# Hybrid attention kernel: row maxima one product a step, their transposition a step later, block ends copied once or on two engines

## The chip, the cores and the metric

The kernel runs on one NeuronCore of a Trainium2 chip. The metric is the device time of one execution in microseconds (us). The core has five engines with queues of their own: TensorE (PE in the rows; PEld is its weight load), VectorE (DVE), ScalarE (ACT), GpSimd (POOL) and SyncE (SP), which issues most DMAs. TensorE writes its products into PSUM, a memory of eight banks, from which VectorE and ScalarE read them.

## The reference

Two layers of a trunk, each with four parallel head groups: grouped-query attention (4 heads of 64), gated linear attention, latent attention (MLA, 4 heads) and a Mamba-2 scan, then one output projection. The change touches only the softmax attention of the first and third group:

```python
def one_block(qblk):
    s = jnp.einsum('bqhgd,bkhd->bhgqk', qblk, k, preferred_element_type=F32) * scale
    p = jax.nn.softmax(s, axis=-1)
    return jnp.einsum('bhgqk,bkhd->bqhgd', p.astype(v.dtype), v)
```

There are 128 context tokens, which read only each other, and 1024 latent tokens, which read 256 cached and 1024 latent keys.

## The kernel before

Each layer first projects all 1152 tokens (the `L267` products), then runs a long stretch in which the eight attention heads go one after the other, with the two scans (tiles `g_...` and `d_...`) spread between them, and ends with the output projection. In the profiled execution the attention stretch is 423 to 872 us in the first layer and 1296 to 1754 us in the second.

**A head.** `attend` works on three blocks of queries: 128 context queries with one chunk of keys, and twice 512 latent queries with ten chunks of 128 keys. A chunk's scores go into a tile `st` (two PSUM banks in turn). Even chunks are exponentiated by ScalarE into `P` (L1117) and multiplied with the values in one product into `po` (L1118). Odd chunks are split into a high part `Ph` and a low part `Pl` (ScalarE L1107 and L1108, VectorE L1110) and take three products (L1112 to L1114). `po` is a single bank: its rows 0 to 63 gather the outputs and row 64 the denominators. At the end of a block ScalarE copies row 64 to `den` (L1127) and rows 0 to 63 into one half of `Ou` (L1129); then the next block may write `po`. After the odd head of a pair the denominators of both heads go through DRAM (`d_den`, `d_rec`), come back as `R`, and scale the pair's outputs (L1143, L1144).

**The maxima.** The scores need each query's maximum over the keys, as two extra rows of `QB`. `maxima` makes them one head ahead: for each of nine query tiles one or three products (L755) into a PSUM tile `mx` (two banks in turn, three for the first head), each reduced by VectorE (L756). After tiles 0, 4 and 8 the group's maxima are negated (L764, L766) and split (L768, L769) into `m`, transposed by TensorE into `mT` (L772) and copied to `QB` by ScalarE (L774).

**The pacing.** All this is written with Python generators. `nxt` gives the preparation of the next head as steps; a head yields 21 times, and after each yield so many steps are traced that all `STEPS[n]` of them are spread evenly over the 21 (`paced` keeps a step behind the head's latest product, exponential and subtraction). For head 0 the steps are driven from `cons_qk` in the last projection, two for each of its 12 tiles. The tile framework's scheduler then sets the order on each engine, so the order in the source is only a priority.

Of the kernel before, what the change touches and what calls it, by code (L numbers as in the profile page):

```python
# [8 lines left out]
F32 = mybir.dt.float32  # L9
# [13 lines left out]
KT = 11  # L23
KEYS = KT * 128
WO_AT, WO_N = 5, 5
STEPS = (13, 19, 13, 25, 22, 20, 19, 0)
EPS = 1e-6


# [5 lines left out]
def hybrid_trunk_kernel(ctx: ExitStack, tc: tile.TileContext, a):  # L35
    nc = tc.nc
    pe, dve, act, pool, sp = nc.tensor, nc.vector, nc.scalar, nc.gpsimd, nc.sync
# [341 lines left out]
    for l in range(L):  # L379
# [83 lines left out]
        with st1:  # L463
# [80 lines left out]
            def gate_out(dst, ch, p):  # L544
                g = wk.tile([128, 384], F32, name="gg", tag="gg", bufs=2)
                act.activation(out=g, in_=p[:, 0:384], func=AF.Tanh, scale=0.5)
                dve.scalar_tensor_tensor(out=g, in0=g, scalar=1.0, in1=p[:, 0:384], op0=ALU.add, op1=ALU.mult)
                sp.dma_start(out=dst[:, ch * 384:(ch + 1) * 384], in_=g)
# [196 lines left out]
            def maxima(sets, mpass, mr, psX=psA):  # L745

                qb = sets[3]
                mx = mxp.tile([128, T, 3], F32, name="mx", tag="mx", bufs=2)
                lt_m, rh_m = mpass
                for t in range(T):  # L750
                    s = slice(t * 128, (t + 1) * 128)
                    cks = ((0, 128),) if t == 0 else ((128, 512), (640, 512), (1152, 256))
                    for i, (o, n) in enumerate(cks):
                        p = psX("mx")
                        pe.matmul(p[:, 0:n], lhsT=lt_m[:, s], rhs=rh_m[:, o:o + n], start=True, stop=True)  # L755
                        dve.tensor_reduce(out=mx[:, t, i:i + 1], in_=p[:, 0:n], axis=AX.X, op=ALU.max)  # L756
                    if t not in (0, 4, 8):
                        yield
                        continue
                    t0 = max(0, t - 3)  # L760
                    n = t + 1 - t0
                    nm = mxp.tile([128, 4], F32, name="nm", tag="nm", bufs=2)
                    if t:
                        dve.tensor_reduce(out=nm[:, 0:n], in_=mx[:, t0:t + 1, :], axis=AX.X, op=ALU.max, negate=True)  # L764
                    else:
                        dve.tensor_scalar(out=nm[:, 0:1], in0=mx[:, 0, 0:1], scalar1=-1.0, scalar2=None, op0=ALU.mult)  # L766
                    m = mxp.tile([128, 4, 2], F32R, name="m", tag="m", bufs=2)
                    dve.tensor_copy(m[:, 0:n, 0:1], nm[:, 0:n].unsqueeze(2))  # L768
                    dve.tensor_tensor(out=m[:, 0:n, 1:2], in0=nm[:, 0:n].unsqueeze(2), in1=m[:, 0:n, 0:1], op=ALU.subtract)  # L769
                    tp = psX("mT")  # L770
                    for i in range(n):
                        pe.matmul(tp[0:2, i * 128:(i + 1) * 128], lhsT=m[:, i, :], rhs=identr, start=(i == 0), stop=(i == n - 1),  # L772
                                  skip_group_check=True)
                    act.copy(qb[mr:mr + 2, t0 * 128:(t0 + n) * 128], tp[0:2, 0:n * 128])  # L774
                    yield
# [52 lines left out]
            def cons_qk(ct, ch, p):  # L828
                if ct < 2:
                    g = wk.tile([128, 384], F32, name="gg", tag="gg", bufs=2)  # L830
                    act.copy(g, p[:, 0:384])
                    sp.dma_start(out=d_qk[ct, :, ch * 384:(ch + 1) * 384], in_=g)
                else:
                    gate_out(d_gt[ct - 2], ch, p)
                for _ in range(2):
                    next(mxs, None)


# [7 lines left out]
        with ExitStack() as sta:  # L846
            sks = ExitStack()
            sk = sks.enter_context(tc.tile_pool(name=f"sk{l}", bufs=1, side=op, reuse_waits="tile"))
            nrm = sta.enter_context(tc.tile_pool(name=f"nrm{l}", bufs=1, side=sd, reuse_waits="tile"))
# [243 lines left out]
            def attend(h, spasses, scale, v, vi, vh, vl, gate_rows, kd, st):  # L1093

                for b, (q0, nq, kts) in enumerate(QBLK):
                    qs = slice(q0, q0 + nq)
                    po = psC("po")
                    for j, kt in enumerate(kts):
                        ks = slice(kt * 128, (kt + 1) * 128)
                        sp_ = psB("st")  # L1100
                        for i, (kx, qx) in enumerate(spasses):
                            anchors["pe"] = pe.matmul(sp_[:, 0:nq], lhsT=kx[:, ks], rhs=qx[:, qs], start=(i == 0), stop=(i == len(spasses) - 1))  # L1102
                        last = j == len(kts) - 1
                        if j % 2:

                            Ph = at.tile([128, 512], F32R, name="Ph", tag="Ph", bufs=3)
                            act.activation(out=Ph[:, 0:nq], in_=sp_[:, 0:nq], func=AF.Exp, scale=scale)  # L1107
                            anchors["act"] = act.activation(out=sp_[:, 0:nq], in_=sp_[:, 0:nq], func=AF.Exp, scale=scale)  # L1108
                            Pl = at.tile([128, 512], F32R, name="Pl", tag="Pl", bufs=2)
                            anchors["dve"] = dve.tensor_tensor(out=Pl[:, 0:nq], in0=sp_[:, 0:nq], in1=Ph[:, 0:nq], op=ALU.subtract)  # L1110
                            k = j // 2
                            pe.matmul(po[0:65, 0:nq], lhsT=vh[:, k, :], rhs=Ph[:, 0:nq], start=False, stop=False, skip_group_check=True)  # L1112
                            pe.matmul(po[0:64, 0:nq], lhsT=vl[:, k, :], rhs=Ph[:, 0:nq], start=False, stop=False, skip_group_check=True)
                            pe.matmul(po[0:65, 0:nq], lhsT=vh[:, k, :], rhs=Pl[:, 0:nq], start=False, stop=last, skip_group_check=True)  # L1114
                        else:
                            P = at.tile([128, 512], F32, name="P", tag="P", bufs=5)
                            anchors["act"] = act.activation(out=P[:, 0:nq], in_=sp_[:, 0:nq], func=AF.Exp, scale=scale)  # L1117
                            pe.matmul(po[0:65, 0:nq], lhsT=v[:, kt, vi, :], rhs=P[:, 0:nq], start=(j == 0), stop=last,  # L1118
                                      skip_group_check=True)
                        if not last:  # L1120
                            yield
                    if h % 2 == 0:
                        st[b] = nrm.tile([128, 512 if b else 128], F32, name=f"Ou{b}", tag=f"Ou{b}")
                    O = st[b]
                    i = h % 2
                    den = nrm.tile([1, 512], F32, name="den", tag="den", bufs=1)
                    act.copy(den[:, 0:nq], po[64:65, 0:nq])  # L1127
                    sp.dma_start(out=d_den[kd, i, qs], in_=den[:, 0:nq])
                    act.copy(O[64 * i:64 * i + 64, 0:nq], po[0:64, 0:nq])  # L1129
                    if i:  # L1130

                        c = nq // 64
                        rc = nrm.tile([128, 8], F32, name="rc", tag="rc", bufs=2)
                        for j in range(2):
                            sp.dma_start(out=rc[64 * j:64 * j + 64, 0:c], in_=d_den[kd, j, qs].rearrange("(p c) -> p c", c=c))
                        dve.reciprocal(out=rc[:, 0:c], in_=rc[:, 0:c])
                        R = nrm.tile([128, 512], F32, name="R", tag="R", bufs=2)
                        for j in range(2):
                            sp.dma_start(out=d_rec[kd, j, qs].rearrange("(p c) -> p c", c=c), in_=rc[64 * j:64 * j + 64, 0:c])
                            sp.dma_start(out=R[64 * j:64 * j + 64, 0:nq], in_=d_rec[kd, j, qs].partition_broadcast(64))  # L1140
                        g = nrm.tile([128, 512], F32, name="gt", tag="gt", bufs=2)
                        sp.dma_start(out=g[:, 0:nq], in_=gate_rows[:, qs])
                        dve.scalar_tensor_tensor(out=g[:, 0:nq], in0=O, scalar=0.5, in1=g[:, 0:nq], op0=ALU.mult, op1=ALU.mult)  # L1143
                        pool.tensor_tensor(out=g[:, 0:nq], in0=g[:, 0:nq], in1=R[:, 0:nq], op=ALU.mult)  # L1144
                        sp.dma_start(out=d_oT[kd, :, qs], in_=g[:, 0:nq])
                    yield
# [105 lines left out]
            for n in range(8):  # L1252
# [14 lines left out]
                if n == 7:  # L1267
                    for k in range(WO_N, KD):
                        load_wo(k)
                total, done = STEPS[n], 0  # L1270
                for j, _ in enumerate(run):
# [209 lines left out]
```

## Time and profile before

| | us |
|---|---|
| time, median of 3 runs | 1841.7 (1835.44 to 1841.74) |
| the profiled execution: its own time | 1836.28 |
| the profiled execution: span from first to last instruction | 1834.5 |
| TensorE busy | 1718.5 (94%) |
| VectorE busy | 1177.2 (64%) |
| ScalarE busy | 859.9 (47%) |
| mean granted TensorE clock | 0.973 |

A busy share is a mean over the span; in the attention stretch VectorE is busier than in the projections. Waits are given as the idle time of an engine in front of an instruction, with the instruction that ended it.

### The profile page before, as it was taken

What the parts mean: (1) busy time and instruction counts of PE and PEld (TensorE: products, weight loads), DVE (VectorE), ACT (ScalarE), POOL (GpSimd) and SP (SyncE); (2) the same over time, 40 slices, a digit from 0 to 9 for tenths busy, and PEclk for the clock granted to TensorE, in tenths of its full rate; (3) what the DMA queues carried; (4) which work ended last, traced back from release to release, by engine and by line L of the source; (5) the groups of instructions that cost most, each with busy time, mean ns of one, the idle gap of its engine ahead of it and who ended that gap; (6) DMA issues with size and microseconds to landing.
All of it is one profiled execution on the core that took longest, in us unless ns stands there. A gap on an engine that the chain in (4) does not pass through costs nothing.

```text
span 1834.5 us, 25155 instructions
## 1 busy us (share of the span) xinstructions
PE 1718.5 (94%) x8200; PEld 1312.8 (72%) x8200; DVE 1177.2 (64%) x2297; ACT 859.9 (47%) x1907; POOL 729.2 (40%) x909
## 2 busy tenths in 40 slices
PE   8999998998998998999999999999999899899998
PEld 2787977896665666656887999889666666565676
DVE  5738887647877886772453447543776788678223
ACT  4634422434654765673442162132465467567322
POOL 3633149824343543330343323871434354333011
PEclk9999988999989999999999999999998999999999
DMA  8435353413323321142433333231442332114243
GB/s 296 138 117 156 113 168 103 129 63 119 115 77 85 90 79 47 41 144 86 138 129 104 102 94 91 60 102 37 122 116 76 81 88 83 50 36 149 87 137 115
DMA packets 179684, 190.99 MB, mean 104 GB/s; under 512 B 29406, under 2 KB 140720, under 8 KB 179552
## 3 DMA queue, kind: packets, MB, share of 16 engines
q1 hardware_dynamic: 174208, 179.11, 32.1%
q10 hardware_dynamic: 5344, 10.26, 1.7%
q8 instruction: 65, 1.06, 0.3%
q14 instruction: 67, 0.55, 0.1%
HBM read 141.00 MB, written 48.30 MB: 103 GB/s over the span
## 4 chain that ended last, share of the span: by engine, by line
PE 54%; DVE 17%; DMA 11%; POOL 7%; issue 5%; ACT 4%; SPq 1%; ACTq 0%; POOLq 0%; DVEq 0%
PE psP L267 19%; PE op L267 8%; PE st L1102 5%; PE po L1118 5%; DMA ast<-in_w_ada_dram 2%; PE mx L755 2%; DMA wst<-in_w_in_dram 2%; DVE mx L756 2%; DVE Pl L1110 2%; PE po L1114 1%; DVE acc L176 1%; DMA R<-d_rec 1%; POOL wlo L261 1%; DVE d_DT L1023 1%; PE go L931 1%
## 5 line engine op out<-in xcount | busy, mean ns | idle before, releaser
L756 DVE TENSOR_REDUCE mx<-mx 128x1 f32<-128x512 f32 (+2 forms) x400 | 224.6, 582 | 92.2 <-PE mx L755 90.6
L267 PE MATMUL psP<-whi,hh 128*128 128x512 f32 (+2 forms) x576 | 202.6, 363 | 6.1 <-DVE whi L257 3.7
L267 PE MATMUL psP<-wlo,hh 128*128 128x512 f32 (+2 forms) x576 | 202.8, 361 | 2.1 <-POOL wlo L261 1.9
L267 PE MATMUL psP<-whi,hl 128*128 128x512 f32 (+2 forms) x576 | 187.5, 359 | 0.1
L261 POOL TENSOR_TENSOR wlo<-wst,whi 128x512 fp32r<-128x512 f32 (+3 forms) x106 | 130.6, 1240 | 137.9 <-DVE whi L257 79.0
L267 PE MATMUL psP<-hh,whi 128*128 128x384 f32 x480 | 163.1, 340 | 4.7 <-DVE whi L257 3.8
L1102 PE MATMUL st<-QA,KA 128*128 128x512 f32 (+1 forms) x336 | 164.0, 488 | 0.6 <-DVE Pl L1110 0.4
L267 PE MATMUL psP<-hl,whi 128*128 128x384 f32 x480 | 160.2, 336 | 0.0
L267 PE MATMUL psP<-hh,wlo 128*128 128x384 f32 x480 | 155.0, 337 | 0.1
L1110 DVE TENSOR_TENSOR Pl<-st,Ph 128x512 fp32r<-128x512 f32 x160 | 109.7, 686 | 65.9 <-ACT st L1108 64.2
L1107 ACT ACTIVATE Ph<-st 128x512 fp32r<-128x512 f32 x160 | 95.5, 597 | 107.5 <-PE st L1102 99.1
L1117 ACT ACTIVATE P<-st 128x512 f32<-128x512 f32 (+1 forms) x176 | 99.8, 567 | 79.1 <-PE st L1102 67.1
L1102 PE MATMUL st<-QB,KB 66*128 66x512 f32 (+3 forms) x336 | 133.0, 401 | 0.0
L267 PEld LDWEIGHTS psP<-whi,hh 128*128 128x128 f32 x576 | 110.3, 193 | 20.3 <-DVE whi L257 5.2
L267 PEld LDWEIGHTS psP<-wlo,hh 128*128 128x128 f32 x576 | 110.4, 193 | 17.9 <-POOL wlo L261 5.3
L267 PEld LDWEIGHTS psP<-whi,hl 128*128 128x128 f32 x576 | 108.5, 192 | 12.4 <-DVE hl L226 0.3
L1102 PEld LDWEIGHTS st<-QA,KA 128*128 128x128 f32 x336 | 65.4, 195 | 49.8 <-issue 39.3
L267 PEld LDWEIGHTS psP<-hh,whi 128*128 128x128 f32 x480 | 90.1, 188 | 12.0 <-DVE whi L257 5.5
L1102 PE MATMUL st<-QB,KA 96*128 96x512 f32 (+1 forms) x168 | 93.2, 555 | 2.1 <-ACT P L1117 1.8
L1108 ACT ACTIVATE st<-st 128x512 f32<-128x512 f32 x160 | 94.8, 592 | 0.0
L1118 PE MATMUL po<-P,vm 128*65 128x512 f32 (+1 forms) x176 | 88.7, 586 | 5.9 <-ACT P L1117 3.4
L1144 POOL TENSOR_TENSOR gt<-gt,R 128x512 f32<-128x512 f32 (+1 forms) x24 | 26.6, 1106 | 166.0 <-DMA R<-d_rec 162.3
(369 smaller groups left out, 4325.2 us busy)
## 6 DMA issues: line engine op xcount, KB each, us to landing
ast<-in_w_ada_dram SPq DMA_DIRECT2D x96, 256.0 KB
wst<-in_w_in_dram SPq DMA_DIRECT2D x64, 256.0 KB
wost<-in_w_out_dram SPq DMA_DIRECT2D x16, 512.0 KB
d_xs<-d_xb SPq DMA_DIRECT2D x32, 192.0 KB
ot<-d_oT SPq DMA_DIRECT2D x18, 320.0 KB
d_tok<-vv SPq DMA_DIRECT2D x18, 256.0 KB
d_gt<-gg SPq DMA_DIRECT2D x24, 192.0 KB
g_qk<-d_qk SPq DMA_DIRECT2D x36, 128.0 KB
```

Source lines behind the costliest of these rows:

```text
L176: dve.scalar_tensor_tensor(out=acc[:, r, :], in0=st, scalar=c, in1=acc[:, r, :], op0=ALU.mult, op1=ALU.add)
L261: eng.tensor_tensor(out=lo[:, 0:n], in0=st[:, 0:n], in1=hi[:, 0:n], op=ALU.subtract)
L267: pe.matmul(p, lhsT=lt, rhs=rh, start=(first and i == 0), stop=(last and i == n - 1))
L755: pe.matmul(p[:, 0:n], lhsT=lt_m[:, s], rhs=rh_m[:, o:o + n], start=True, stop=True)
L756: dve.tensor_reduce(out=mx[:, t, i:i + 1], in_=p[:, 0:n], axis=AX.X, op=ALU.max)
L1102: anchors["pe"] = pe.matmul(sp_[:, 0:nq], lhsT=kx[:, ks], rhs=qx[:, qs], start=(i == 0), stop=(i == len(spasses) - 1))
L1107: act.activation(out=Ph[:, 0:nq], in_=sp_[:, 0:nq], func=AF.Exp, scale=scale)
L1108: anchors["act"] = act.activation(out=sp_[:, 0:nq], in_=sp_[:, 0:nq], func=AF.Exp, scale=scale)
L1110: anchors["dve"] = dve.tensor_tensor(out=Pl[:, 0:nq], in0=sp_[:, 0:nq], in1=Ph[:, 0:nq], op=ALU.subtract)
L1117: anchors["act"] = act.activation(out=P[:, 0:nq], in_=sp_[:, 0:nq], func=AF.Exp, scale=scale)
L1118: pe.matmul(po[0:65, 0:nq], lhsT=v[:, kt, vi, :], rhs=P[:, 0:nq], start=(j == 0), stop=last, skip_group_check=True)
L1144: pool.tensor_tensor(out=g[:, 0:nq], in0=g[:, 0:nq], in1=R[:, 0:nq], op=ALU.mult)
```

## The change

`maxima` yields after every product and no longer after every query tile, and once more between the split and the transposition. `STEPS` is raised to the new number of steps of each head, and `cons_qk` drives three steps per tile. At the end of a block an even head copies rows 0 to 64 of `po` in one ScalarE copy, and its denominators leave from row 64 of `Ou`; an odd head copies the outputs on ScalarE and the denominators on VectorE.

```diff
-STEPS = (13, 19, 13, 25, 22, 20, 19, 0)
+STEPS = (35, 41, 35, 45, 44, 41, 41, 0)
...
                         dve.tensor_reduce(out=mx[:, t, i:i + 1], in_=p[:, 0:n], axis=AX.X, op=ALU.max)
+                        yield
                     if t not in (0, 4, 8):
-                        yield
                         continue
...
                     dve.tensor_tensor(out=m[:, 0:n, 1:2], in0=nm[:, 0:n].unsqueeze(2), in1=m[:, 0:n, 0:1], op=ALU.subtract)
+                    yield
                     tp = psX("mT")
...
-                for _ in range(2):
+                for _ in range(3):
                     next(mxs, None)
...
-                    den = nrm.tile([1, 512], F32, name="den", tag="den", bufs=1)
-                    act.copy(den[:, 0:nq], po[64:65, 0:nq])
+                    if i:
+                        den = nrm.tile([1, 512], F32, name="den", tag="den", bufs=1)
+                        act.copy(O[64:128, 0:nq], po[0:64, 0:nq])
+                        dve.tensor_copy(den[:, 0:nq], po[64:65, 0:nq])
+                    else:
+
+                        act.copy(O[0:65, 0:nq], po[0:65, 0:nq])
+                        den = O[64:65, :]
                     sp.dma_start(out=d_den[kd, i, qs], in_=den[:, 0:nq])
-                    act.copy(O[64 * i:64 * i + 64, 0:nq], po[0:64, 0:nq])
```

In the changed file the lines behind the first edits have moved: L772 is L773 there, L1102 is L1103, L1053 is L1054, L1118 is L1119.

**First place: the last maxima of head 5 (head 5 itself is running, head 6 is being prepared).** On TensorE, before, from the group's last product `mx` 128x256 to the transposition:

```order
L755 MATMUL mx<-KA_4247,QB_4250 128x256
L931 MATMUL go<-g_v_5634,g_A_4252 128x64 x4
L931 MATMUL go<-g_v_5653,g_A_4251 128x64 x4
L772 MATMUL mT<-identr,m 2x128 x4
L1112 MATMUL po<-Ph,vh 65x512
```

On TensorE, after, the end of the same stretch (it begins 30 products ahead of the transposition; `vm` are value products of head 6's preparation):

```order
L1115 MATMUL po<-Pl,vh 65x512
L1214 MATMUL vm<-wuhl,ckh 128x128 x2
L1214 MATMUL vm<-wuhl,ckl 128x128
L1214 MATMUL vm<-wuhl,ckh 128x128
L1103 MATMUL st<-QB_4250,KA_4247 128x512
L1103 MATMUL st<-QA_4249,KA_4247 128x512
L1103 MATMUL st<-QB_4250,KB_4248 128x512
L932 MATMUL go<-g_v_5653,g_A_4251 128x64 x4
L1103 MATMUL st<-QB_4250,KA_4247 128x512
L1103 MATMUL st<-QA_4249,KA_4247 128x512
L1103 MATMUL st<-QB_4250,KB_4248 128x512
L773 MATMUL mT<-identr,m 2x128 x4
```

On VectorE, before, at the same place (`nm` and `m` are the group's maxima, `d_y` the output sum of the Mamba scan):

```order
L756 TENSOR_REDUCE mx<-mx 128x1 x2
L764 TENSOR_REDUCE nm<-mx 128x4
L1053 TENSOR_TENSOR d_y<-dy,d_y 128x256
L768 CAST m<-nm 128x4
L1054 SCALAR_TENSOR_TENSOR d_y<-d_y,d_sz 128x256
L769 TENSOR_TENSOR m<-nm,m 128x4
```

On VectorE, after:

```order
L756 TENSOR_REDUCE mx<-mx 128x1
L764 TENSOR_REDUCE nm<-mx 128x4
L768 CAST m<-nm 128x4
L1047 TENSOR_TENSOR d_yi<-dyi,ec 128x256
L769 TENSOR_TENSOR m<-nm,m 128x4
L1054 TENSOR_TENSOR d_y<-dy,d_y 128x256
```

So the transposition now has 30 products in front of it where it had 8 small ones, and the split of the maxima has moved from behind the first `d_y` sum to ahead of it.

**Second place: the last maxima of head 3 (head 3 itself is running, head 4 is being prepared).** On TensorE, before (`krT` are transposed keys of head 4, `cum` belongs to a scan):

```order
L755 MATMUL mx<-KA_4247,QA_4249 128x512
L1118 MATMUL po<-P,vg 65x512
L1102 MATMUL st<-QA_4249,KA_4247 128x512
L1102 MATMUL st<-QB_4250,KB_4248 128x512
L887 MATMUL cum<-gcum,g_lg_5140 128x131
L755 MATMUL mx<-KA_4247,QA_4249 128x512
L755 MATMUL mx<-KA_4247,QA_4249 128x256
L1176 MATMUL krT<-ident,krt 32x128 x3
L1112 MATMUL po<-Ph,vh 65x512
L1113 MATMUL po<-Ph,vl 64x512
L755 MATMUL mx<-KA_4247,QA_4249 128x512 x2
```

On TensorE, after, at the same place:

```order
L755 MATMUL mx<-KA_4247,QA_4249 128x512
L888 MATMUL cum<-gcum,g_lg_5140 128x131
L755 MATMUL mx<-KA_4247,QA_4249 128x256
L1119 MATMUL po<-P,vg 65x512
L1103 MATMUL st<-QA_4249,KA_4247 128x512
L1103 MATMUL st<-QB_4250,KB_4248 128x512
L755 MATMUL mx<-KA_4247,QA_4249 128x512
L1103 MATMUL st<-QA_4249,KA_4247 128x512
L1103 MATMUL st<-QB_4250,KB_4248 128x512
L755 MATMUL mx<-KA_4247,QA_4249 128x512
L1113 MATMUL po<-Ph,vh 65x512
L1114 MATMUL po<-Ph,vl 64x512
```

Before, two products of maxima directly behind each other are followed by three short transpositions and two value products, and then by two more products of maxima; now the last two that are shown stand singly, with score products ahead of each.

**Third place: the end of head 1's last block, an odd head.** On ScalarE, before (what a row waits for is named behind it by engine):

```order
L904 COPY g_ktk<-kT 128x128 [waits PE_49]
L1127 COPY den<-po 1x512 [waits DMAHW6_49,PE_49]
L1129 COPY Ou_6235<-po 64x512
L1127 COPY den<-po 1x128 [waits DMAHW2_49,PE_49]
L1129 COPY Ou_6612<-po 64x128
```

On ScalarE, after:

```order
L982 DMA o_ssd_dram<-d_hs 128x128 [waits DMAHW7_49,Activation_49]
L1129 COPY Ou_6231<-po 64x512 [waits PE_49]
L890 ACTIVATE g_E_4722<-cum 128x131 [waits PE_49]
L892 ACTIVATE g_Ei_4724<-cum 128x128
L905 COPY g_ktk<-kT 128x128 [waits PE_49]
L1133 COPY Ou_6606<-po 65x128 [waits PE_49]
```

On VectorE, after, where the denominators' copy is new:

```order
L895 TENSOR_TENSOR g_kq_4730<-g_qk_4702,g_Ei_4712 128x128 [waits Activation_49]
L1024 TENSOR_SCALAR d_DT<-tri,dtv 128x128 [waits DVE_49]
L1024 TENSOR_SCALAR d_DT<-tri,dtv 128x128 x3
L756 TENSOR_REDUCE mx<-mx 128x1 [waits PE_49]
L1130 COPY den<-po 1x512 [waits DMAHW0_49,Activation_49]
L1149 SCALAR_TENSOR_TENSOR gt<-Ou_6231,gt 128x512 [waits DMAHW3_49,DMAHW2_49,Pool_49]
L896 SCALAR_TENSOR_TENSOR g_kq_4741<-g_qk_4714,g_E_4722 128x128 [waits DMAHW6_49,Activation_49]
```

ScalarE has one copy fewer at each block end, and on VectorE the denominators' copy stands behind a reduction and waits for a count of ScalarE (`Activation`), not for one of TensorE.

## Rows read from the trace of the kernel before

**Rows 1.** The page's head and busy times: share of the span, instructions.

```profile
span 1834.5 us, 25155 instructions
...
PE 1718.5 (94%) x8200; PEld 1312.8 (72%) x8200; DVE 1177.2 (64%) x2297; ACT 859.9 (47%) x1907; POOL 729.2 (40%) x909
```

**Rows 2.** Attention stretches: length, busy PE, PEld, DVE, ACT, POOL (instructions), clock, DMA.

```profile
423.00:872.00 449.00, 413.33 (x1812) 276.77 (x1812) 328.77 (x717) 266.78 (x568) 170.62 (x206) 0.97 0.30 89
1296.00:1754.00 458.00, 423.51 (x1846) 283.95 (x1845) 326.22 (x719) 268.80 (x571) 173.77 (x206) 0.96 0.31 91
```

**Rows 3.** Waits of PE, first layer's attention: total us, times, longest us.

```profile
PE mx L755 <- DVE mx L756: 7.4, 10, 2.9
PE po L1114 <- DVE Pl L1110: 7.3, 7, 3.0
PE mT L772 <- DVE m L769: 3.9, 3, 2.9
PE po L1118 <- ACT Ou L1129: 3.8, 5, 1.5
```

**Rows 4.** Waits of PE, second layer's attention.

```profile
PE mx L755 <- DVE mx L756: 7.4, 9, 3.0
PE po L1114 <- DVE Pl L1110: 6.7, 8, 2.1
PE mT L772 <- DVE m L769: 4.9, 4, 2.8
...
PE po L1118 <- ACT Ou L1129: 2.3, 4, 1.0
```

**Rows 5.** Timeline at head 5's last maxima: start, duration, engine, [idle before <-releaser].

```profile
722.45 0.42 DVE L1053 TENSOR_TENSOR d_y<-dy,d_y 128x256 f32<-128x256 f32 x1 [2.33 <-POOL d_y L1048]
...
722.79 0.34 DVE L768 CAST m<-nm 128x4 fp32r<-128x4 f32 x1
...
723.38 0.15 DVE L769 TENSOR_TENSOR m<-nm,m 128x4 fp32r<-128x4 f32 x1
...
723.58 0.59 PE L772 MATMUL mT<-identr,m 128*2 128x128 f32 x4 [2.87 <-DVE m L769]
```

**Rows 6.** Timeline at head 3's last maxima.

```profile
595.06 0.72 POOL L1048 TENSOR_TENSOR d_y<-d_y,d_yi 128x256 f32<-128x256 f32 x1
...
595.81 0.42 DVE L1053 TENSOR_TENSOR d_y<-dy,d_y 128x256 f32<-128x256 f32 x1 [2.53 <-POOL d_y L1048]
596.15 1.01 DVE L756 TENSOR_REDUCE mx<-mx 128x1 f32<-128x512 f32 x2
...
596.89 0.83 PE L755 MATMUL mx<-KA,QA 128*128 128x512 f32 x2 [2.87 <-DVE mx L756]
```

**Rows 7.** Timeline at the end of head 1's last block.

```profile
514.45 0.46 PE L755 MATMUL mx<-KA,QA 128*128 128x512 f32 x1
...
517.74 0.68 DVE L756 TENSOR_REDUCE mx<-mx 128x1 f32<-128x512 f32 x1
...
519.55 0.58 ACT L1127 COPY den<-po 1x512 f32<-1x512 f32 x1 [3.06 <-PE po L1114]
...
520.16 0.58 ACT L1129 COPY Ou<-po 64x512 f32<-64x512 f32 x1
...
520.79 0.69 PE L1118 MATMUL po<-P,vg 128*65 128x128 f32 x2 [1.04 <-ACT Ou L1129]
```

**Rows 8.** Stretches at granted clock 0.50: sum over four of them, then over eight.

```profile
sum 23.80, PE 18.12 PEld 10.59 DVE 13.60 ACT 15.84 POOL 13.62; mean PE 4.53 PEld 2.65 DVE 3.40 ACT 3.96 POOL 3.40
...
sum 51.20, PE 43.79 PEld 28.98 DVE 31.35 ACT 26.71 POOL 25.71; mean PE 5.47 PEld 3.62 DVE 3.92 ACT 3.34 POOL 3.21
```

**Rows 9.** Copies of a block end, and a VectorE sum from PSUM: ns min/median/max.

```profile
L1127 ACT COPY den<-po x48: 258/578/582, 427.0 to 1752.8; 1x512 f32<-1x512 f32 x32, 1x128 f32<-1x128 f32 x16
...
L1129 ACT COPY Ou<-po x48: 257/578/582, 427.3 to 1753.4; 64x512 f32<-64x512 f32 x32, 64x128 f32<-64x128 f32 x16
...
L184 DVE TENSOR_TENSOR gr<-ada,gr x4: 671/678/679, 132.6 to 423.4; 2x512 f32<-2x512 f32 x4
```

## The prediction

> **What bounds the kernel now.** I read the page first. TensorE is busy for 94% of the span, VectorE for 64%, ScalarE for 47% [rows 1]: TensorE sets the time, and a change that removes no product can gain only its idle time and its time at a low clock. The windows of the two attention stretches come second [rows 2]. TensorE is idle there for 449.0 - 413.3 = 35.7 us and 458.0 - 423.5 = 34.5 us, 70 us in all, and VectorE, at 64% over the span, is busy for 73% and 71%. So VectorE has less slack here than the page says. Third, the table of TensorE's waits, by what ended them [rows 3, 4]. Four kinds matter for this change. Products of maxima that wait for an earlier reduction cost 7.4 + 7.4 = 14.8 us, transpositions that wait for the split `m` 3.9 + 4.9 = 8.8 us, the first value product of a block that waits for the `Ou` copy 3.8 + 2.3 = 6.1 us. These 29.7 us are what the change can address. The fourth kind, value products that wait for `Pl` (7.3 + 6.7 = 14.0 us), is not touched by it, but depends on the same VectorE.
>
> The largest of these waits are few: one of 2.9 and one of 2.8 us for the transposition, one of 2.9 and one of 3.0 us for the maxima. The timeline says where they lie in the first layer. At head 5's last maxima VectorE stood still for 2.33 us, because the sum of `d_y` ahead of the split in its queue waited for GpSimd. The split came after it, and TensorE waited 2.87 us for the split [rows 5]. At head 3's last maxima the same sum held VectorE for 2.53 us, two reductions stood behind it, and two products in the two banks waited 2.87 us [rows 6]. So the stall is not VectorE's work but a queue in order: a sum that waits for GpSimd has maxima behind it.
>
> Last, the clock. Four stretches, two in each layer, at a granted clock of 0.50 (the level of 1.2 GHz) follow these four stalls: the one at 721.0 us begins inside the 2.87 us wait of the transposition, the one at 598.1 us directly after the wait of the maxima. They sum to 23.80 us with 18.12 us of busy TensorE. All eight such stretches in attention ahead of the last head sum to 51.20 us with 43.79 us busy [rows 8]. At full clock half of the busy time would be saved: 9.1 us of the four, 21.9 us of the eight.
>
> **The change, part by part.** *The transposition a step later.* At head 5's last maxima the order shows two moves that help: the split now stands ahead of the `d_y` sum on VectorE, and the transposition has 30 products in front of it where it had 8 small ones. The longest wait of each layer should go: -2.9 - 2.8 = -5.7 us [rows 3, 4]. Bounds: 0, if another instruction that waits for GpSimd gets ahead of the split, and -8.8, if all transposition waits go. The smaller ones I leave in, since a transposition still follows soon on the split elsewhere. `d_y` is late next, by the 0.34 + 0.15 us of the split, and it was late already for GpSimd's sake.
>
> *One product of maxima a step.* At head 3's last maxima the pairs of products are pulled apart by score products, so a bank has more time to be read: -2.9 - 3.0 = -5.9 us [rows 3, 4]. Bounds: 0 and -14.8. I do not take more, because the schedule had spread the products before: over the whole program, about as many products of maxima stand directly behind another of their kind after the change as before.
>
> *The clock behind these stalls.* If the four stalls go, the four stretches should go with them: -9.1 us [rows 8]; bounds 0 and -21.9.
>
> *Even heads' block ends.* One copy of 65 rows takes the place of two. The copies of 1x512 and of 64x512 both take 578 ns [rows 9]: rows cost nothing, so I price 65 rows at 578 ns, and the bank comes free 0.58 us sooner. There are 16 such ends with 512 queries, but most of the `Ou` wait is not there. I take -1.5 us, of bounds 0 and -4 (two thirds of the 6.1 us).
>
> *Odd heads' block ends.* Outputs now on ScalarE, denominators on VectorE. By the diff the two could run together, but in the order VectorE's copy waits for a count of ScalarE, that of the output copy, so they run one after the other as before: 0.58 us on ScalarE, then a copy on VectorE, plus VectorE's queue. The trace has no VectorE copy of this shape; the nearest row is its sum of 2x512 from PSUM, 0.68 us [rows 9]. At the end of head 1's last block the next block's product waited 1.04 us for the two ScalarE copies [rows 7]. At this time VectorE reduced a product (514.45, 0.46 long) at 517.74 only, 2.8 us behind. If its copy meets that lag, the bank comes free up to 2.8 us later than now; if VectorE is idle, 0.1 us later. TensorE mostly has scores and scan products to do meanwhile. I take 1.0 us at this end in each layer, +2 us, of bounds 0 and 2.8 us at each of 16 ends.
>
> The Trainium skill ("PSUM — Partial Sum Buffer", "PSUM bank collisions raise a hardware error") lets two engines use one bank at the same time if they stay in different quadrants of 32 partitions, which rows 0 to 63 and row 64 do. By that rule the split copy would free the bank of an odd head some 0.58 us sooner, and the sum would come out about 3 us lower; the order's rows, with their wait on ScalarE, speak against it, and no run shown here has two engines in one bank.
>
> *Load on VectorE.* It gets 32 copies at about 0.68 us and 16 short ones, which I put at 0.27 us by ScalarE's short copy of 0.26: 26 us on 328.8 + 326.2 = 655 us in attention, 4% [rows 2, 9]. What waits for VectorE (14.8 + 8.8 + 14.0 = 37.6 us) should grow by as much: +1.5 us. Behind the odd copy on VectorE stand `gt`, `g_kq`, `d_DT` and the reductions; the scans wait for the first ones, the maxima for the last.
>
> *What the new order brings.* All instructions of the heads are reshuffled, and the kernel has some 70 us of idle TensorE in many small waits that can fall in new places, the sum of `d_y` behind GpSimd above all. I take back a third of the three gains above (5.7 + 5.9 + 9.1 = 20.7): +7 us; bounds 0 and all of it.
>
> *At nothing:* three steps per tile in the projection, whose products lie among hundreds of `L267` products ready to run (uncovered, 1.01 us for two reductions at a few of the 12 tiles [rows 6]); the denominators' DMAs, 48 as before and behind no new wait but the copy's; ScalarE's saved copies, 26 us on an engine with half its time free.
>
> The sum: -5.7 - 5.9 - 9.1 - 1.5 + 2 + 1.5 + 7 = -11.7 us. The profiled execution took 1836.3 us, which gives 1824.6. The median of the runs is 5.4 us above it and the lowest run 0.8 below, so I name 1827, half of that difference above the sum.
>
> **Rivals.** *The stalls only move* (no change). For it: the cause is a VectorE sum that waits for GpSimd, which the change does not remove, and the scheduler had already spread the products. If something else, `Pl` or a scan product, stands behind the sum in place of the maxima, TensorE waits as long and the clock falls as before: 1835 to 1841. Against it: at head 5 the order does put the split ahead of that sum.
>
> *The odd heads' copy on VectorE comes late* (slower). Place: the 16 ends with 512 queries of heads 1, 3, 5 and 7. Price: the bank is held for VectorE's lag, up to 2.8 us [rows 7]; at half of it less what is covered, 1.3 us x 16 = 21 us, and one stretch at 0.50 in each layer, 5.5 us busy each [rows 8], half of it lost: +5. With the gains of 20 us reduced to the transposition and half of the rest, about -14, that is +12: 1848, 0.65% above the profiled execution. It decides once VectorE's lag at a block end exceeds the scores and scan products that TensorE has left. For it: VectorE is over 70% busy and a single bank `po` joins the blocks. Against it: `Ou` waits were 9 in all, so most ends are covered.
>
> *All of the three waits vanish, with the clock behind them* (much faster): -29.7 and up to -21.9. With most of the wait and little clock beyond the four stretches, about -33: 1803. Against it: ten and nine waits of maxima lie in many places, and neighbours of that kind are as many as before.
>
> **How the numbers follow.** Forecast (gain of 6 to 22 us, 1815 to 1832): 0.45. Stalls only move: 0.30. Copy late: 0.13. All vanish: 0.12. A measurement of this kernel can tell about 0.5%, 9.2 us, from no change. Of the forecast's 0.45, 0.07 lies within that; with 0.30 of the first rival, same 0.37. Faster: 0.38 + 0.12 = 0.50; slower 0.13. The range takes in the forecast, the first rival, most of the second and some of the third: 1805 to 1847.
>
> **What would show it.** Right: no wait of the transposition over 1 us at head 5, none of maxima near 3 us at head 3, two to four stretches at 0.50 fewer in attention, idle TensorE there near 60 us. Even ends: one copy of about 0.58 us. Odd ends: VectorE's copy begins only when ScalarE's has ended; if they overlap, that step is wrong. The first rival shows in waits for `Pl`, `dy` or `go` that grow as the others shrink; the second in waits of `po` for `den` of over 1 us at many odd ends; the third in a clock close to 1.00 in both stretches. The forecast is wrong if the four stretches at 0.50 appear elsewhere, since they and the stalls ahead of them are the whole gain.

## The result and the profile after

The changed kernel takes 1861.7 us (median of 4 runs, 1855.6 to 1864.6) against 1839.8 us of the kernel before, measured beside it: 1.2% slower, ratio 1.0122 with a 95% interval of 1.0092 to 1.0152. The forecast was 1827 us, in a range of 1805 to 1847. The profiled execution has a span of 1853.8 us, 19.3 us more than before [rows 1]. Its page:

```profile
span 1853.8 us, 25076 instructions
...
PE 1723.4 (93%) x8200; PEld 1319.4 (71%) x8200; DVE 1205.7 (65%) x2321; ACT 837.8 (45%) x1859; POOL 729.7 (39%) x909
```

The work is the same and moved as meant: ScalarE has 22 us less, VectorE 28 us more. Of the 19.3 us 15.6 lie in the two attention stretches. These are their windows, from the first block's end of head 0 to the last block's end of head 7 in each layer, first of the changed kernel, then of the kernel before (columns as in [rows 2]):

```profile
430.00:881.90 451.90, 416.08 (x1830) 280.87 (x1831) 335.27 (x725) 253.23 (x538) 170.07 (x200) 0.97 0.30 89
1298.80:1771.90 473.10, 428.08 (x1827) 288.98 (x1827) 338.84 (x725) 255.65 (x541) 169.82 (x204) 0.94 0.29 87
```

```profile
427.60:881.70 454.10, 419.87 (x1838) 282.21 (x1839) 328.16 (x716) 265.98 (x564) 169.74 (x201) 0.97 0.30 89
1298.70:1754.00 455.30, 420.85 (x1833) 282.25 (x1832) 324.28 (x716) 266.62 (x565) 172.50 (x204) 0.96 0.30 91
```

The first layer's stretch is 2.2 us shorter than before, the second's 17.8 us longer: TensorE is idle for 45.0 us there instead of 34.5, and busy for 7.2 us more with the same products. The longer busy time fits the clock. Five stretches of the second layer at a granted clock of 0.50 (1.2 GHz) became ten; half of the busy time in them is 14.9 us before and 25.1 us after (window sums, the kernel before first):

```profile
sum 34.00, PE 29.83 PEld 19.03 DVE 20.76 ACT 17.08 POOL 12.84; mean PE 5.97 PEld 3.81 DVE 4.15 ACT 3.42 POOL 2.57
```

```profile
sum 54.40, PE 50.12 PEld 34.80 DVE 34.29 ACT 19.58 POOL 11.79; mean PE 5.01 PEld 3.48 DVE 3.43 ACT 1.96 POOL 1.18
```

In the first layer five such stretches became seven, with 25 to 26 us of busy TensorE in them before and after.

The waits of TensorE in the two stretches of the changed kernel answer to [rows 3, 4] (lines 773, 1115, 1119 are 772, 1114, 1118 there); first layer, then second:

```profile
PE mT L773 <- DVE m L769: 9.6, 6, 5.0
PE po L1115 <- DVE Pl L1111: 5.2, 6, 1.4
...
PE po L1119 <- DVE den L1130: 2.5, 2, 2.3
PE mx L755 <- DVE mx L756: 2.5, 5, 1.4
```

```profile
PE mT L773 <- DVE m L769: 6.4, 5, 3.4
PE po L1119 <- ACT P L1118: 4.6, 3, 3.8
PE po L1115 <- DVE nm L766: 4.1, 1, 4.1
PE po L1115 <- DVE Pl L1111: 3.8, 2, 2.0
PE go L932 <- DVE d_yi L1047: 3.2, 1, 3.2
...
PE mx L755 <- DVE mx L756: 3.1, 7, 0.9
...
PE po L1119 <- DVE den L1130: 2.4, 3, 1.8
```

One kind of wait was exchanged for another. Waits of the products of maxima fell from 14.8 to 5.6 us, as the single products should do. Waits for the split, which the transposition's extra step should have cut, rose from 8.8 to 16.0 us. Waits for the odd denominators (4.9 us) took the place of those for `Ou` (6.1 us before). The rest is spread over products that the change doesn't touch.

The copies of a block end cost what was assumed: 65 rows in 580 ns, VectorE's copy of the denominators in 685 ns (minimum, median, maximum):

```profile
L1130 DVE COPY den<-po x24: 285/685/687, 478.7 to 1771.9; 1x512 f32<-1x512 f32 x16, 1x128 f32<-1x128 f32 x8
...
  ACT Ou L1129: 17.6, 6
...
  PE po L1119: 4.9, 5
```

```profile
L1133 ACT COPY Ou<-po x24: 258/580/586, 429.7 to 1704.2; 65x512 f32<-65x512 f32 x16, 65x128 f32<-65x128 f32 x8
```

In the group of VectorE's copy the second row is the idle time of VectorE ahead of it, until ScalarE's copy was done, the third the time that TensorE waited for it. All 24 began after ScalarE's copy had ended, between 0.03 and 4.1 us later.

### The profile page after: what moved, and what is told of

Its sections match the earlier page's. It is cut to its first block, busy times and chain, and to the rows that moved or that the text cites. A ratio compares the mean times of both kernels' runs of the same rounds, so it can differ in the third digit from the quotient of the medians.

```text
span 1853.8 us, 25076 instructions
## 1 busy us (share of the span) xinstructions
PE 1723.4 (93%) x8200; PEld 1319.4 (71%) x8200; DVE 1205.7 (65%) x2321; ACT 837.8 (45%) x1859; POOL 729.7 (39%) x909
## 4 chain that ended last, share of the span: by engine, by line
PE 57%; DVE 15%; DMA 11%; POOL 8%; issue 5%; ACT 4%; SPq 1%; POOLq 0%; DVEq 0%; ACTq 0%
PE psP L267 18%; PE op L267 9%; PE st L1103 6%; PE po L1119 5%; PE mx L755 3%; DMA ast<-in_w_ada_dram 2%; DMA wst<-in_w_in_dram 2%; PE po L1115 1%; POOL wlo L261 1%; PE att L911 1%; DVE mx L756 1%; PE go L932 1%; PE po L1113 1%; PE po L1114 1%; POOL sq L622 1%
## 5 line engine op out<-in xcount | busy, mean ns | idle before, releaser
L1103 PE MATMUL st<-QA,KA 128*128 128x512 f32 (+1 forms) x336 | 160.5, 478 | 2.2 <-ACT P L1118 2.2
L1118 ACT ACTIVATE P<-st 128x512 f32<-128x512 f32 (+1 forms) x176 | 99.7, 567 | 85.2 <-PE st L1103 83.3
L1103 PE MATMUL st<-QB,KB 66*128 66x512 f32 (+3 forms) x336 | 133.1, 400 | 0.0
L1103 PEld LDWEIGHTS st<-QA,KA 128*128 128x128 f32 x336 | 65.7, 196 | 50.0 <-issue 37.0
L1103 PE MATMUL st<-QB,KA 96*128 96x512 f32 (+1 forms) x168 | 96.6, 575 | 4.1 <-DVE Pl L1111 1.4
L1119 PE MATMUL po<-P,vm 128*65 128x512 f32 (+1 forms) x176 | 89.5, 590 | 6.7 <-ACT P L1118 4.7
L1119 PE MATMUL po<-P,vg 128*65 128x512 f32 (+1 forms) x176 | 88.2, 583 | 4.9 <-DVE den L1130 4.1
```

## Experiments

Theory A: the new pacing of the maxima costs. Theory B: the odd heads' denominators on VectorE come late (the second rival). Theory C: the cost is the new order of all instructions, whoever causes it. Theory D came up later, that a step for each product finishes the other preparation of the next head too early.

**One part at a time, and an edit without a purpose.** Four kernels, each scheduled anew: the maxima part alone; the block ends alone; of the ends the odd heads alone; and the kernel before with each head's number of steps raised by one.

```diff
-STEPS = (13, 19, 13, 25, 22, 20, 19, 0)
+STEPS = (14, 20, 14, 26, 23, 21, 20, 0)
```

Maxima alone: 

> The change's maxima part alone (a step per product, a step before the transposition, STEPS raised, three steps per tile in the projection); block ends as before. If the new pacing of the maxima is what costs (theory A): 1.008 to 1.014 of the kernel before, with waits of the transposition for the split near the 16 us of the whole change (8.8 before). If the odd heads' denominators on VectorE are what costs (theory B): 0.990 to 1.000, with waits of the transposition near 9 us. If it is only the reshuffling of all instructions (theory C): anywhere between 0.993 and 1.012, and the parts do not add up to the whole.

Ends alone: 

> The change's block ends alone (even heads one copy, odd heads outputs on ScalarE and denominators on VectorE); maxima as before. Theory A: 0.996 to 1.002. Theory B: 1.008 to 1.014, with waits of the next block's products for the odd denominators well over 6 us. Theory C: between 0.993 and 1.012, and the waits for the denominators do not explain it.

Odd heads alone: 

> Of the block ends, the odd heads alone (outputs on ScalarE, denominators on VectorE); even heads and maxima as before. Theory A: 0.998 to 1.003. Theory B: 1.008 to 1.014, as the block ends together or slightly more. Theory C: anywhere between 0.993 and 1.012.

One step more: 

> The kernel before with every head's STEPS raised by one and nothing else: the same work and the same copies, only the preparation runs slightly ahead. It measures how much a reshuffling without a purpose moves the time. Theories A and B: within 0.3% of before. Theory C: off by 0.5% or more, in either direction.

Measured: 1.0139 (1.0105 to 1.0172), 1.0199 (1.0175 to 1.0222), 1.0170 (1.0142 to 1.0197) and 1.0190 (1.0149 to 1.0231). Each part alone costs no less than both together, and so does the edit that changes no work at all. That speaks for theory C and against A; B is left open by the second and third. All three theories missed somewhere: the first three times lie above the 1.012 that theory C allowed. The first lies in theory A's range, but its waits for the split are 10.8 us, not near 16; the second lies above theory B's range with 4.8 us of waits for the denominators, not well over 6. Waits don't tell the kernels apart either: with one step more, waits for the split fell to 2.7 us, the least of the four, and the kernel is 1.9% slower. In the kernel with the odd heads alone no product of TensorE waits for VectorE's denominators, yet it is 1.7% slower.

**The order held fixed.** The scheduler can be taken out by edges between neighbours on each engine's queue, which set the issue order and nothing else. With the order of the kernel before listed for each engine, one thing is changed at a time: in the traces of these kernels TensorE, VectorE, ScalarE and GpSimd issue in the order of before but for the edits named.

```python
for p, q in zip(ranks, ranks[1:]):
    tc.add_manual_dep(xs[q], xs[p].name, mybir.DependencyInfo(
        mybir.DependencyClass.NoSync, mybir.DependencyReason.DATA), reason="order")
```

The change's block ends in the old order: 

> The change's block ends, with the issue order of every engine fixed by edges to that of the kernel before (the dropped copies of denominators left out, VectorE's new copies free to be placed). Nothing else is reshuffled. If the block ends themselves cost (theory B): 1.010 or more. If the reshuffling costs (theory C): 0.996 to 1.003; the prediction's own terms for the ends (-1.5 + 2 + 1.5 us) give 1.001.

Measured: 1.0145 (1.0117 to 1.0173). Theory B, left open so far, holds in this order. At the end of head 5's second block (timeline; VectorE's queue from the end of ScalarE's copy to the next block's first product):

```profile
754.39 0.58 ACT L1128 COPY Ou<-po 64x512 f32<-64x512 f32 x1
754.59 0.99 DVE L1220 TENSOR_TENSOR QA<-qr,QB 32x384 fp32r<-32x384 f32 x1
...
757.87 1.28 DVE L756 TENSOR_REDUCE mx<-mx 128x1 f32<-128x512 f32 x2
759.07 0.68 DVE L1110 TENSOR_TENSOR Pl<-st,Ph 128x512 fp32r<-128x512 f32 x1
...
760.80 0.69 DVE L1129 COPY den<-po 1x512 f32<-1x512 f32 x1
...
761.54 1.97 PE L1118 MATMUL po<-P,vm 128*65 128x512 f32 x2 [6.48 <-DVE den L1129]
```

The outputs are out of the bank at 754.97, the denominators wait in VectorE's queue until 760.80, and TensorE stands for 6.48 us. The waits of TensorE, first layer and second:

```profile
PE po L1118 <- DVE den L1129: 11.3, 5, 6.5
```

```profile
PE po L1118 <- DVE den L1129: 11.4, 5, 6.5
```

That is 22.7 us where the copies to `Ou` had cost 6.1 us, close to the 21 us that the second rival gave, though in ten waits of up to 6.5 us and not in sixteen of 1.3. So the odd copy is harmful by itself in this order, and a scheduler that knows of it can buy its way out: in the changed kernel TensorE waits 4.9 us for it, but VectorE stands idle ahead of six of the copies for 17.6 us (the row above).

Even heads alone in the old order: 

> The kernel before with its order fixed on every engine; only the even heads' ends are the change's (one ScalarE copy of 65 rows, the dropped copies left out of the order). The prediction's term: -1.5 us of 0 to -4, so 0.998 to 1.000. A theory by which the copies of a block end cost whatever they are would give 1.005 or more.

Measured: 0.9983 (0.9964 to 1.0003). One copy in place of two is worth about 3 us, within the bounds, and hardly to be told from nothing. By difference the odd heads' part costs some 1.6% in that order.

The new order with the old ends: 

> The order of the changed kernel fixed on every engine, but with the block ends of before (ScalarE copies the denominators directly ahead of the outputs, nothing on VectorE). Theory B (the odd ends on VectorE cost): 0.996 to 1.003 of the kernel before. Theory C (the order costs, whoever makes it): 1.009 to 1.016, as the changed kernel.

Measured: 1.0131 (1.0106 to 1.0155), the same as the changed kernel. In the new order the block ends cost nothing that shows, and the order alone makes the loss.

**The four stalls, taken out by hand.** In the order of before, VectorE's queue at head 5's last maxima is changed as the scheduler had changed it:

```diff
-L1053 TENSOR_TENSOR d_y<-dy,d_y 128x256
 L768 CAST m<-nm 128x4
-L1054 SCALAR_TENSOR_TENSOR d_y<-d_y,d_sz 128x256
 L769 TENSOR_TENSOR m<-nm,m 128x4
+L1053 TENSOR_TENSOR d_y<-dy,d_y 128x256
+L1054 SCALAR_TENSOR_TENSOR d_y<-d_y,d_sz 128x256
 L1110 TENSOR_TENSOR Pl<-st,Ph 128x512
```

> The kernel before with its order fixed, but for one move in each layer: at head 5's last maxima the split of the maxima stands ahead of the sum of d_y on VectorE. The prediction's step (the wait of 2.9 and 2.8 us goes, with the stretch at granted clock 0.50 behind it, 2.1 + 2.4 us): -10 us, 0.994 to 0.996. If the stall only moves (next in VectorE's queue behind that sum is Pl, which a value product needs): 0.998 to 1.001, with a wait for Pl of 1.5 to 2.5 us at the same place.

Measured: 1.0009 (0.9991 to 1.0028). The timeline shows the stall move as the first rival had it:

```profile
725.24 0.40 PE L772 MATMUL mT<-identr,m 128*2 128x128 f32 x4 [0.24 <-DVE m L769]
726.08 0.44 PE L1112 MATMUL po<-Ph,vh 128*65 128x512 f32 x1 [0.44 <-ACT Ph L1107]
...
726.79 0.42 DVE L1053 TENSOR_TENSOR d_y<-dy,d_y 128x256 f32<-128x256 f32 x1 [1.60 <-POOL d_y L1048]
...
728.38 0.69 PE L1114 MATMUL po<-Pl,vh 128*65 128x512 f32 x1 [1.62 <-DVE Pl L1110]
```

The transposition waits 0.24 us where it waited 2.87; three products later TensorE waits 1.62 us for `Pl`, which now stands behind the sum. So the sum was put behind `Pl` too, and at head 3 behind both reductions:

> As the one before, and more: at head 5 Pl too stands ahead of the sum of d_y, and at head 3's last maxima both reductions stand ahead of it, in both layers. If a sum that waits for GpSimd with TensorE's work behind it is the cause of these four stalls: they go, -11.6 us, with the four stretches at 0.50, -9.1 us: 0.988 to 0.991. If stalls and low clock only move: 0.996 to 1.001.

Measured: 0.9994 (0.9978 to 1.0009). Waits of this kernel, first layer, then second:

```profile
PE po L1114 <- DVE Pl L1110: 10.6, 8, 3.0
PE mx L755 <- DVE mx L756: 4.8, 10, 1.6
...
PE mT L772 <- DVE m L769: 2.0, 4, 0.8
```

```profile
PE po L1114 <- DVE Pl L1110: 10.2, 9, 2.9
PE mx L755 <- DVE mx L756: 4.3, 8, 1.6
...
PE mT L772 <- DVE m L769: 2.1, 4, 1.0
```

The waits of maxima and transpositions fell from 23.6 to 13.2 us, as foreseen; those for `Pl` rose from 14.0 to 20.8 us. Of 10.4 us taken away 6.8 came back in one neighbour, and the time did not change. Over the whole span of the profiled execution TensorE was idle for 121.1 us, where it had been 116.0. The low clock stayed too: at each of the four places a stretch at 0.50 still begins, at 599.8, 729.5, 1473.6 and 1596.5 us. Their window sum, to be compared with the first of [rows 8]:

```profile
sum 17.00, PE 16.62 PEld 10.34 DVE 8.49 ACT 7.25 POOL 7.12; mean PE 4.16 PEld 2.58 DVE 2.12 ACT 1.81 POOL 1.78
```

TensorE is busy in them for 16.62 us, where it had been 18.12. The granted clock is 0.976 at the median of this kernel's runs, and 0.975 at that of the kernel before, measured beside it.

Both harmless parts together: 

> The kernel before with its order fixed, even heads in one copy, and the sum of d_y behind the split, Pl and the reductions at heads 3 and 5 (two earlier kernels in one). If their effects add (-0.2% and -0.1%): 0.996 to 0.998. If the waits are shared: 0.998 to 1.001.

Measured: 0.9979 (0.9960 to 0.9999), 1835.3 us, the lowest ratio here, by an amount that barely shows.

**Is it the pace, and how small may the edit be?** Three kernels scheduled anew, with block ends as before. In the first the yields of one query tile count together as one step (`wt` is 1 over their number), so that only the products of a tile are pulled apart; the second has the transposition's step alone; in the third one head has one step more.

```diff
-                        yield
+                        yield wt
...
-                        done += 1
+                        done += paced(steps) or 1
```

Same pace: 

> The change's maxima part (single products, transposition apart) with weighted steps: the yields of one query tile count together as one step, STEPS, the two steps per projection tile and the other preparation as before, block ends as before. So nothing but the products of a tile is pulled apart. If the change costs because a step per product finishes all other preparation of the next head in the first third of its maxima (theory D): 0.995 to 1.003. If every new order costs, with whatever pace (theory C): 1.008 to 1.02.

Transposition's step alone: 

> The kernel before with the transposition's extra step alone (STEPS raised by three), products and block ends as before. By the prediction's step: 0.994 to 0.998, with waits of the transposition for the split of 3 us or less in place of 8.8. Theory C: 1.008 to 1.02, whatever these waits become. Theory D: 0.997 to 1.003, since the other preparation is hardly moved.

Head 6 alone: 

> The kernel before with STEPS of head 6 alone raised from 19 to 20: the smallest edit without a purpose. If a new order costs only where the edit lies: 1.000 to 1.003. If it spreads through the whole program (theory C): 1.008 to 1.02. Theory D: 1.000.

Measured: 1.0106 (1.0075 to 1.0137), 1.0089 (1.0061 to 1.0116), 1.0047 (1.0029 to 1.0064). Theory D falls: with the old pace the maxima part still costs 1.1%. The transposition's step by itself left 8.1 us of waits for the split, not 3, and cost 0.9%. Even the smallest edit costs 0.5%, less than theory C had it. In its profiled execution the attention stretches are no longer than before (450.4 and 454.8 us, against 454.1 and 455.3); its loss lies outside these windows, and no experiment followed it there.

**One order, twice.** In the trace of the kernel before, the two layers' attention has nearly the same order on TensorE: some 40 of the first layer's 1838 products have no match in the second's order. In the changed kernel some 700 of 1830 have none, and the loss lies in the second layer. (Unlike layers are not needed for a loss: in the kernel with one step more they agree as before, and both are slower, 472.2 and 474.7 us.) So the changed kernel was run with the first layer's order in both layers, and with the second's in both.

> The changed kernel, block ends and all, with the order of every engine fixed, and in the second layer's attention stretch the order that the scheduler gave the first layer's (452.0 us long against 473.1). If the loss lies in the particular order of the second layer and not in what the change does (theory C): 20 us less, 0.997 to 1.004 of the kernel before. If the second layer is slower for another reason (data, transfers, or the change's own work): 1.009 to 1.014.

> The reverse: the changed kernel with the second layer's order in both attention stretches. Theory C: the first layer slows by about 20 us too, 1.020 to 1.025. Otherwise 1.009 to 1.014.

Measured: 1.0081 (1.0060 to 1.0102) and 1.0212 (1.0186 to 1.0239). The same instructions with the same data differ by 1.3% (1853.8 against 1877.3 us) through their order alone. The attention stretches of the two, the first layer's order first:

```profile
427.90:885.00 457.10, 419.85 (x1830) 283.13 (x1831) 337.68 (x725) 253.89 (x538) 171.55 (x200) 0.96 0.29 88
1310.40:1773.60 463.20, 420.60 (x1822) 282.79 (x1823) 335.86 (x723) 252.32 (x536) 171.04 (x199) 0.96 0.29 88
```

```profile
427.60:906.10 478.50, 431.76 (x1837) 291.43 (x1836) 343.10 (x727) 256.95 (x544) 173.44 (x206) 0.94 0.28 85
1324.90:1799.90 475.00, 428.03 (x1826) 288.88 (x1826) 340.23 (x725) 255.72 (x542) 169.59 (x204) 0.94 0.29 87
```

With the second layer's order the first layer goes from 451.9 to 478.5 us; with the first layer's, the second goes from 473.1 to 463.2. That is all of theory C one way, and half of it the other way: 1.0081 is not the 0.997 to 1.004 expected. Such a length is good to some 5 us only: the first layer's stretch, whose order was kept, took 457.1 us here and 451.9 in the changed kernel.

At the start of attention the first layer's order has the longest wait of the changed kernel, 5.0 us for the split, which stands behind the decay matrices on VectorE. In the last kernel it stands ahead of them:

> As the kernel with the first layer's order twice, and at the start of attention the split of the maxima stands ahead of the decay matrices (d_DT) on VectorE, behind which the transposition waited 5.0 us. If this wait is time lost: 5 to 10 us less than that kernel, 0.992 to 1.000. If it only moves to another wait: within 0.2% of that kernel.

Measured: 1.0055 (1.0034 to 1.0076), by the medians 4.4 us less than the kernel with the same order otherwise. Of its timeline, the start of attention in the first layer:

```profile
429.08 0.40 PE L773 MATMUL mT<-identr,m 128*2 128x128 f32 x4 [1.93 <-DVE m L769]
434.20 0.44 PE L1115 MATMUL po<-Pl,vh 128*65 128x512 f32 x1 [2.94 <-DVE nm L766]
```

The transposition waits 1.93 us, and 2.05 in the second layer, where it waited 5.02 and 5.13; the next product of `Pl` now waits 2.94 and 1.14 us where it did not. Of 6.2 us 4.1 came back within 5 us. Measured side by side, the six times of this kernel have a mean 4.7 us below that of the six of the other, with a 95% interval of 1.8 to 7.6 us. So some gain is shown; whether it is the 5 us or more of time lost or the 0.2% (3.7 us) or less of a wait that moved, is not.

## Why the prediction was wrong

- **What bounds the kernel:** right for the changed kernel. Most of its loss lies in TensorE's idle time and low clock in attention, and VectorE is what TensorE mostly waits for there.
- **The step that failed is "What the new order brings":** it took back 7 us, and at most the three gains, 20.7 us, so what hangs on the order was to come to -13.7 us. With the ends of before the order alone costs 1.31% of 1837.5 us, 24 us. I had priced the four stalls that the new order removes and treated the rest of it as a rebate on them, when seven other new orders cost between 0.5% and 2.0%, two of them made by an edit without a purpose. Over the whole program the order before is better than any that the scheduler made here anew; why, and whether by luck, nothing here tells.
- **The transposition, the maxima and the clock behind them, -20.7 us:** wrong even where nothing else moves: -0.06%, with an interval of -0.22 to +0.09%. The first rival's mechanism, "the stalls only move", describes these four places, down to `Pl` as the next in the queue; I had named it, and gave it 0.30. The stretches at 0.50 did not go with the waits: the 18.12 us of busy TensorE in them fell to 16.62.
- **The transposition a step later:** in the changed kernel its waits nearly doubled, from 8.8 to 16.0 us. An extra step in the source is only a priority, and at head 5 I misread the new order: it shows `d_yi` (L1047) between the two halves of the split, L768 and L769, and I looked only at the sum of `d_y`, which stands behind both. Like that sum, `d_yi` waits for GpSimd. In the first layer the second half of the split stands behind it, in the second layer the product `go` waits for it (timeline of the changed kernel):

```profile
734.45 0.42 DVE L1047 TENSOR_TENSOR d_yi<-dyi,ec 128x256 f32<-128x256 f32 x1 [2.46 <-POOL d_y L1049]
...
734.79 0.33 DVE L769 TENSOR_TENSOR m<-nm,m 128x4 fp32r<-128x4 f32 x1
...
735.17 0.40 PE L773 MATMUL mT<-identr,m 128*2 128x128 f32 x4 [2.06 <-DVE m L769]
```

```profile
1606.84 0.42 DVE L1047 TENSOR_TENSOR d_yi<-dyi,ec 128x256 f32<-128x256 f32 x1 [3.26 <-POOL d_y L1049]
...
1607.41 3.65 PE L932 MATMUL go<-g_v,g_A 128*128 128x64 f32 x16 [3.16 <-DVE d_yi L1047]
```

So the stall of 2.87 us at head 5 became one of 2.06 us, with a stretch at 0.50 from 736.3 us on, and that of 2.85 us in the second layer one of 3.16 us, with a stretch from 1606.7 us on. This is the condition that the lower bound named (another instruction that waits for GpSimd ahead of the split) and the sign of the first rival. The longest wait, 5.02 us, arose at the start of attention.
- **One product of maxima a step, -5.9 us:** right as a wait. Waits of maxima fell by 9.2 us, and none is near 3 us any more (the longest 1.4); the time does not show it.
- **Odd heads, +2 us:** mis-sized for the old order, where the odd copies make 22.7 us of waits. The second rival's place and mechanism were right there, and its price in the sum; in the changed kernel it is not what costs, since its order with the old ends is as slow.
- **Copies in series:** right. The two engines never read the bank at once, so the rule that would have let them (the Trainium skill, "PSUM — Partial Sum Buffer", "PSUM bank collisions raise a hardware error") was not put to use; no run here shows two engines in one bank.
- **Even heads, -1.5 us:** right within the measurement (about -3 us).
- **VectorE's load, +1.5 us:** its 26 us were summed wrongly, over the copies of all heads. Only the odd heads' moved, 24 copies, 13 us together by their row above. That the page shows 28 us more is luck: the rest is unchanged instructions that took longer, and with the maxima part alone, without a copy on VectorE, the page already shows 22 us more (1199.5). Its share in the loss was not measured by itself.

What stays open: which property makes one order 1 to 2% better than another. What the slower kernels share is more idle time of TensorE, by their pages (span less busy time) between 124.2 us with one step more for head 6 and 144.6 us with the second layer's order twice, where the kernel before has 116.0. No single wait accounts for it. The kernel with one step more has the fewest waits for the split of all that were scheduled anew and is among the slowest, and giving the second layer the first's order won back only half of its loss.

## What to carry to other kernels

Where a scheduler sets the order, the first experiment is an edit without a purpose, and the second is the change with the old order held by edges: the one shows how far a new order alone can move the time, the other what the change does in the old order. A stall that is removed in an in-order queue may only move to the next instruction that isn't ready, as these did. Look at what stands behind the late one before counting it, and count the low clock behind it as gone only where that next wait is gone too. Read a new order for every instruction that waits for the late engine, not only for the one that stood in the way before. A small copy moved to a busy engine frees a bank only when that engine's queue gets to it.

## What the runs showed of the hardware

A cast of 128x4 on VectorE, 0.17 us at the median, took 2.48 us at the start of attention in the changed kernel (timeline of VectorE, GpSimd and TensorE):

```profile
426.43 1.96 POOL L814 TENSOR_TENSOR QA<-qT,QA 64x384 fp32r<-64x384 f32 x2 [0.77 <-ACT QA L813]
...
426.94 2.95 DVE L1024 TENSOR_SCALAR d_DT<-tri,dtv 128x128 f32<-128x128 f32 x1
...
427.43 2.48 DVE L768 CAST m<-nm 128x4 fp32r<-128x4 f32 x1
...
429.26 0.56 POOL L969 MEMSET d_H<- 128x256 f32 x2
...
429.87 1.04 POOL L1014 TENSOR_TENSOR d_R<-avh,tri 128x512 fp32r<-128x512 f32 x1
...
433.18 0.59 PE L773 MATMUL mT<-identr,m 128*2 128x128 f32 x4 [5.02 <-DVE m L769]
```

The decay matrix `d_DT` ahead of it in the queue was as slow, 2.95 us, and ended at 429.89; the cast ended at 429.91. GpSimd worked without a gap of 0.1 us from 426.43 on; its memsets ended at 429.82, and its next instruction began at 429.87. In the last kernel, with no `d_DT` ahead, the cast took 2.78 us and ended at 428.83, where GpSimd's memsets ended at 428.79 and its next instruction began at 428.86. The Trainium skill ("SBUF — State Buffer", "Who interferes with whom") says that a cast of VectorE in a two-port mode and GpSimd lock each other out of a port pair that they share, for the whole instruction of the one that issues first. The common ends agree with a lock, but the cast waited past several of GpSimd's instructions, none of them longer than about 1 us. No row tells whether this cast runs in such a mode, and no run here tried it by itself.
